# A gated decoder block: w_pool's products among two gates' products, one weight sum per step, first head's blocks issued behind x

## The chip, the cores and the metric

The kernel runs on one core of one Trainium2 chip. The metric is the device time of one launch in microseconds (us), the median of several runs. The engines are named as in the profile: PE (TensorE, matmuls; PEld is its weight load), DVE (VectorE), ACT (ScalarE), POOL (GpSimd) and SP (SyncE, which here only issues transfers).

## The reference

One block of a decoder, sequence 1024, width 1024, all in float32. Cut to what matters:

```python
proj = x @ w_in                                 # 1024 x 7168
q, f_pre, i_val, o_gate, pool_v, gate_a, gate_b = split(proj)
o = hgrn2_chunked(silu(q) * scale, 1 - f, i_val, log(f))      # f from f_pre; 8 heads, chunks of 16
a = (rms_norm(o) * hgrn_norm_g * sigmoid(o_gate)) @ w_a
pooled = causal_multiscale_pool(pool_v)         # trailing means over 2, 4, 8, 16 tokens, minus the token
b = einsum('bsgc,gcd->bsgd', pooled, w_pool) * pool_scale     # 4 groups of 256 columns
merged = sigmoid(gate_a) * a + sigmoid(gate_b) * b
x = LN(alpha * x + merged @ w_out)
x = LN(alpha * x + relu(x @ w_up) ** 2 @ w_down)
```

## The kernel before

**Products.** Every float32 operand is split into a high part, rounded to the fast float32 format of PE (an ACT copy, L125), and a low part, the rest (a DVE subtraction, L126). A product of two such pairs takes three matmuls: L211, L213 and L214 in `prod`, L112, L113 and L114 in `mm3`. Tiles are 128 x 512: sequence halves `u` of 512 tokens, blocks of 128 columns.

**Seven products for eight.** A pair of column blocks of a weight matrix is multiplied with Strassen's scheme in Winograd's form, in `pair`: seven products p1 to p7 instead of eight, of 4 x 3 matmuls each, from sums of weight blocks (b11, b12, b21, b22 and a fifth tile, t) on one side and sums of x on the other. Each step has an operand (t0, b_21, t2, t3, t1, t4, b_22, in that order, which makes the sum and splits it) and a product (p1, p2, p6, p7, p5, p4, p3). Where two pairs run side by side ("twin") the order is another. The sums s1 to s4 of x and their parts (`xp`) stay in SBUF. `takes` say what becomes of the four results.

**Stages.** `head_inputs(h)` makes q and f of a head, `output_gates(h)` the output gates, `pooled(g)` the pooled values of a group (to DRAM, po), `gates(j)` the two gates ga and gb of column block j (to DRAM). They run in the order of the table `ORDER`, one `pair` each. Beside them runs the recurrence of the heads, a generator: `run` calls it once after each product (`next(turning[0])`), and it puts out a piece of a half head. A half head's output is turned (transposes L990, DVE L992 into tile `og`) and written by `put_output`, in part with accumulating stores on POOL's queue (L637).

**The stage in question.** The last in `ORDER` is the sixth gates, `gates(6)`. Behind it stood the four `pool_products(g)` and `gates(7)`. `pool_products(g)` loads w_pool's group and four tiles of pooled values into the ring of six "raw" tiles, which also takes the weight blocks, splits them (group's parts to the rooms q and f, pooled values to the ring "w" of ten), loads gb of the block into one of the rooms v, q, f and og, makes four products of 2 x 3 matmuls, multiplies each with scale and gate (L751) and stores pb. For column block 7, whose gate is not there yet, the scaled product is stored (L749) and `gates(7)` loads it again and multiplies (L722).

**Who sets the order.** The order on PE in this part is the program's own. On the other engines a scheduler of the tile framework sets it, by when operands and tiles are ready in its model and by priorities; every engine then runs its list in order. All loads and most stores are issued by SP, in order: a transfer whose tile is not free yet holds all behind it. A tile of a ring is free when its last reader, a store's landing included, is done.

## Time and profile before

| | us |
|---|---|
| median of three runs | 1473.27 (1473.22 to 1474.59) |
| the profiled execution | 1472.62 |
| its span in the trace | 1470.8 |
| PE busy | 1438.0 |
| DVE busy | 1100.2 |
| ACT busy | 760.8 |

The span is what the trace covers; 1.8 us of the execution's own time lie around it. The sixth gates' first product begins at 600.73 us of the span, w_pool's first at 620.3, the seventh gates' first at 651.43. Views that group or sum the trace name lines of this kernel (L12 is line 12), tiles without their numbers, and count an engine's idle time to what ended it. A matmul is shown with its whole latency of 0.39 us, though the next one may start before it ends.

### The profile page before, as it was taken

Reading aid. Unit: us, or ns where it says so; the run is one execution under the profiler, and the core shown is the slowest. Engines: PE = TensorE matmul, PEld = TensorE weight load, DVE = VectorE, ACT = ScalarE, POOL = GpSimd, SP = SyncE. Lnnn points to the kernel's source line nnn. Section 1 sums busy time; section 2 is a strip of 40 time slices with the busy share of each in tenths; the row PEclk is TensorE's granted clock in tenths of the full one; section 3 lists DMA queues with packets and bytes.
Section 4 is the critical chain, followed back from the end, with each engine's and each line's share of the span. In section 5 each row is a group of like instructions: output and inputs, shape, how many; then the busy total and the mean of one; then the engine's idle time right before and its main releaser. Section 6 shows DMA issues by size and latency. Waiting matters only on the chain.

```text
span 1470.8 us, 20899 instructions
## 1 busy us (share of the span) xinstructions
PE 1438.0 (98%) x7377; PEld 1189.8 (81%) x7377; DVE 1100.2 (75%) x1807; ACT 760.8 (52%) x1383; POOL 107.4 (7%) x288
## 2 busy tenths in 40 slices
PE   8999999999999999979999999999999999999997
PEld 7788888788878888858788878888888888888886
DVE  4967876896897796467985598566666787777977
ACT  5545566665755655545542366555556543333435
POOL 0002111211211210000002100000000100000000
PEclk9999999999999999989999999999999999999999
DMA  7142245345435536797663134444447874435422
GB/s 258 58 136 87 76 127 165 79 137 152 107 93 145 136 87 174 247 337 256 223 230 114 58 100 174 137 154 156 144 151 264 275 263 150 163 131 170 129 72 115
DMA packets 187738, 229.21 MB, mean 156 GB/s; under 512 B 12240, under 2 KB 110576, under 8 KB 187632
## 3 DMA queue, kind: packets, MB, share of 16 engines
q1 hardware_dynamic: 181664, 213.96, 43.9%
q0 software_dynamic: 5184, 11.54, 4.0%
q10 hardware_dynamic: 784, 2.38, 0.5%
q8 instruction: 58, 0.95, 0.3%
q14 instruction: 48, 0.39, 0.1%
HBM read 150.22 MB, written 77.59 MB: 155 GB/s over the span
## 4 chain that ended last, share of the span: by engine, by line
PE 88%; DVE 5%; DMA 4%; issue 1%; ACT 1%; SPq 0%; POOL 0%; DVEq 0%; ACTq 0%
PE ps_pj L211 15%; PE ps_pj L214 15%; PE ps_pj L213 15%; PE ps_pj L1369 4%; PE ps_pj L1367 4%; PE ps_pj L1368 4%; PE ps_pj L112 2%; PE ps_pj L113 2%; PE ps_pj L114 2%; PE ps_tr L1369 1%; PE ps_tr L1367 1%; PE ps_tr L1368 1%; PE ps_sc L211 1%; PE ps_sc L213 1%; PE ps_sc L214 1%
## 5 line engine op out<-in xcount | busy, mean ns | idle before, releaser
L211 PE MATMUL ps_pj<-act,w 128*128 128x512 f32 x1068 | 420.5, 394 | 8.3 <-ACT c L274 2.9
L214 PE MATMUL ps_pj<-act,w 128*128 128x512 f32 x1068 | 416.0, 391 | 2.3 <-DVE w L126 2.3
L213 PE MATMUL ps_pj<-act,w 128*128 128x512 f32 x1068 | 415.3, 390 | 0.0
L125 ACT CAST w<-raw 128x512 fp32r<-128x512 f32 x326 | 202.3, 622 | 289.8 <-PE ps_pj L213 200.9
L126 DVE TENSOR_TENSOR w<-raw,w 128x512 fp32r<-128x512 f32 x326 | 222.8, 686 | 107.2 <-ACT w L125 101.0
L211 PEld LDWEIGHTS ps_pj<-act,w 128*128 128x128 f32 x1068 | 200.9, 188 | 53.6 <-ACT c L274 4.5
L214 PEld LDWEIGHTS ps_pj<-act,w 128*128 128x128 f32 x1068 | 200.8, 188 | 46.4 <-DVE w L126 3.9
L213 PEld LDWEIGHTS ps_pj<-act,w 128*128 128x128 f32 x1068 | 201.0, 188 | 40.5
L1329 ACT CAST act<-act 128x1024 fp32r<-128x1024 f32 x66 | 67.1, 1050 | 109.0 <-issue 35.0
L278 DVE TENSOR_TENSOR c<-c,ps_pj 128x512 f32<-128x512 f32 x95 | 64.7, 682 | 43.5 <-PE ps_pj L214 41.5
L1368 PE MATMUL ps_pj<-act,act 128*128 128x512 f32 x240 | 93.0, 389 | 0.0
L1369 PE MATMUL ps_pj<-act,act 128*128 128x512 f32 x240 | 93.0, 389 | 0.0
L1330 DVE TENSOR_TENSOR act<-act,act 128x1024 fp32r<-128x1024 f32 x66 | 79.4, 1219 | 17.6 <-ACT act L1329 16.5
L1367 PE MATMUL ps_pj<-act,act 128*128 128x512 f32 x240 | 92.5, 389 | 0.0
L274 ACT COPY c<-ps_pj 128x512 f32<-128x512 f32 x96 | 55.9, 582 | 2.5 <-DMA v<-c 1.3
L1368 PEld LDWEIGHTS ps_pj<-act,act 128*128 128x128 f32 x240 | 45.0, 188 | 9.4
L1369 PEld LDWEIGHTS ps_pj<-act,act 128*128 128x128 f32 x240 | 45.0, 188 | 9.4
L1367 PEld LDWEIGHTS ps_pj<-act,act 128*128 128x128 f32 x240 | 45.0, 188 | 9.3
L283 DVE TENSOR_TENSOR raw<-raw,raw 128x512 f32<-128x512 f32 x43 | 29.6, 689 | 28.2 <-DMA raw<-in_w_in_dram 27.1
L1238 ACT ACTIVATE c<-c 128x512 f32<-128x512 f32 x61 | 38.5, 632 | 1.7
L1237 ACT ACTIVATE c<-c 128x512 f32<-128x512 f32 x46 | 29.1, 632 | 16.6 <-DVE c L278 16.4
L1323 DVE TENSOR_TENSOR act<-act,ps_pj 128x512 f32<-128x512 f32 x45 | 30.1, 681 | 6.0 <-PE ps_pj L1369 5.7
(413 smaller groups left out, 2664.2 us busy)
## 6 DMA issues: line engine op xcount, KB each, us to landing
h<-c SPq DMA_DIRECT2D x106, 256.0 KB, 2.7
raw<-in_w_in_dram SPq DMA_DIRECT2D x100, 256.0 KB, 3.2
act<-h SPq DMA_DIRECT2D x78, 256.0 KB, 3.0
draw<-in_w_down_dram SPq DMA_DIRECT2D x16, 1024.0 KB, 7.7
raw<-in_w_up_dram SPq DMA_DIRECT2D x56, 256.0 KB, 2.8
hf<-h SPq DMA_DIRECT2D x34, 256.0 KB, 3.0
s<-og POOLq DMA_DIRECT2D x28, 256.0 KB, 6.1
v<-v SPq DMA_DIRECT2D x16, 256.0 KB, 3.5
```

What stands on the lines that cost most here:

```text
L125: A.copy(hi, src)
L126: V.tensor_sub(lo, src, f(hi))
L211: PE.matmul(ps, wh[:, k], th, start=first and k == 0, stop=False, skip_group_check=True)
L213: PE.matmul(ps, wh[:, k], tl, start=False, stop=False, skip_group_check=True)
L214: PE.matmul(ps, wl[:, k], th, start=False, stop=k == CH - 1, skip_group_check=True)
L274: A.copy(t, ps)
L278: V.tensor_add(t, t, ps)
L1329: A.copy(hi, src)
L1330: V.tensor_sub(lo, src, f(hi))
L1367: PE.matmul(ps, hh[:, w], wh, start=fresh and n == 0, stop=False, skip_group_check=True)
L1368: PE.matmul(ps, hh[:, w], wl, start=False, stop=False, skip_group_check=True)
L1369: PE.matmul(ps, hl[:, w], wh, start=False, stop=n == M - 1, skip_group_check=True)
```

## The change

Three things change.

1. `pool_products` becomes one generator over all groups. While the sixth and seventh gates run, `turning[0]` is `beside(stream, counts)`, which after each of a gate's products steps the remaining recurrence and then as many pool products as `POOL_AFTER` says: 1, 1, 1, 1, 1, 1, 2 in the sixth gates, 2, 2, 2, 2, 0, 0, 0 in the seventh. The tiles come from rooms of the recurrence: w_pool's block to tC, its parts to the ring tD, tE, tF, og, the pooled values to the ring tA, tA, st, st, tH, tH, gb to the four f tiles. The result is in the PSUM tag "tr", two banks. Block 7's scaled products stay in the two v tiles and `gates(7)` multiplies by them there.
2. In `pair`, `make_t2` made two sums in step t2 (L290, L291); now it makes one, and the other is made in step t1, both from other operands than before.
3. The first head's weight blocks are issued behind the last load of x.

```diff
@@ -33,8 +33,9 @@
 ORDER = (
     ("inputs", 1), ("pooled", 0), ("inputs", 2), ("gates", 0), ("output_gates", 2), ("inputs", 3), ("pooled", 1),
     ("inputs", 4), ("output_gates", 4), ("gates", 1), ("inputs", 5), ("pooled", 2), ("inputs", 6), ("output_gates", 6),
-    ("gates", 2), ("inputs", 7), ("pooled", 3), ("gates", 3), ("gates", 4), ("gates", 5), ("gates", 6),
+    ("gates", 2), ("inputs", 7), ("pooled", 3), ("gates", 3), ("gates", 4), ("gates", 5),
 )
+POOL_AFTER = {6: (1, 1, 1, 1, 1, 1, 2), 7: (2, 2, 2, 2, 0, 0, 0)}
 PRIO_WHOLE = 6000
 QUARTER = HALF // 2
 PRIO = 60
@@ -282,14 +283,6 @@
             c["t"] = block_tile() if t is None else t
             V.tensor_sub(c["t"], b22, b12)
 
-        def make_t2():
-            if turned:
-                V.tensor_sub(b12, b11, b12)
-                minus_sum(b11, b22, b12)
-            else:
-                V.tensor_sub(b12, b12, b11)
-                V.tensor_sub(b11, b22, b12)
-
         def t3():
             if twin:
                 make_t3()
@@ -300,6 +293,12 @@
                 make_t3()
                 make_t2()
             return w_part(b11)
+
+        def make_t2():
+            if turned:
+                minus_sum(b11, c["t"], b11)
+            else:
+                V.tensor_add(b11, c["t"], b11)
 
         def t4():
             if twin:
@@ -311,6 +310,10 @@
             return w_part(b21)
 
         def t1():
+            if turned:
+                minus_sum(b12, b22, b11)
+            else:
+                V.tensor_sub(b12, b22, b11)
             return w_part(b12)
 
         def p1(w):
@@ -455,7 +458,7 @@
 
         def load_x(u, w):
             rows_of = x2[u * HALF : (u + 1) * HALF, w].rearrange("(t p) c -> p t c", p=P)
-            nc.sync.dma_start(out=x_rows[u][:, :, w], in_=rows_of)
+            return nc.sync.dma_start(out=x_rows[u][:, :, w], in_=rows_of)
 
         def act_rows():
             return [f(act_tile()) for _ in range(2)]
@@ -486,7 +489,7 @@
         load_x(1, slice(0, HALF))
         load_block(b22, 1, 1)
         load_block(b12, 0, 1)
-        load_x(1, slice(HALF, D))
+        last_x = load_x(1, slice(HALF, D))
         b11, b22, b21, b12 = (rows_of_block(t) for t in blocks)
 
         def parts(rows):
@@ -686,8 +689,10 @@
                     V.scalar_tensor_tensor(t, src, QSCALE, t, ALU.mult, ALU.mult)
                 return take
 
+            with tc.issue_after(last_x.ins) if not h else nullcontext():
+                blocks = loaded_blocks(w_in, h * P, D + h * P)
             run(pair(
-                loaded_blocks(w_in, h * P, D + h * P), (c_soon, c_late, room_f),
+                blocks, (c_soon, c_late, room_f),
                 (take_q(0), take_f(0), take_q(1), take_f(1)),
             ), behind=behind)
 
@@ -710,46 +715,83 @@
             ))
 
         def gates(j):
-            spare = j == KT - 1
-            rooms = [lambda tag=tag: tt(tag) for tag in ("q", "f", "og")] if spare else (c_soon, c_late, c_late)
-
-            def take(dst, src=None, more=None):
+            final = j == KT - 1
+            room = (lambda: tt("q")) if final else c_late
+
+            def take(dst, src=None, u=None):
                 def put(t):
-                    s = (tt("v") if spare else c_late()) if src else t
-                    more_of = loaded(more, lambda: tt("v")) if more is not None else None
+                    s = (tt("og") if final else c_late()) if src else t
                     A.activation(s, t, AF.Sigmoid)
-                    if more_of is not None:
-                        V.tensor_mul(s, s, more_of)
-                    nc.sync.dma_start(out=dst if more is None else more, in_=s)
+                    if final and u is not None:
+                        V.tensor_mul(s, s, held[u])
+                    nc.sync.dma_start(out=pbd[j][u] if final and u is not None else dst, in_=s)
                 return put
 
-            more = pbd[j] if spare else (None, None)
             run(pair(
-                loaded_blocks(w_in, 5 * D + j * P, 6 * D + j * P), rooms,
-                (take(gad[j][0]), take(gbd[j][0], True, more[0]), take(gad[j][1]), take(gbd[j][1], False, more[1])),
+                loaded_blocks(w_in, 5 * D + j * P, 6 * D + j * P), (room if final else c_soon, room, room),
+                (take(gad[j][0]), take(gbd[j][0], True, 0), take(gad[j][1]), take(gbd[j][1], False, 1)),
             ))
 
-        def pool_products(g):
-
-            rooms = iter(("v", "q", "f", "og"))
-            raw = loaded(w_pool[g].rearrange("(k p) c -> p k c", p=P), lambda: block_tile((2, 2 * P)))
-            pods = [[loaded(pod[2 * g + i][u], lambda: block_tile((HALF,))) for i in range(2)] for u in range(2)]
-            parts = iter(("q", "f"))
-            wh, wl = split(raw, lambda: tt(next(parts), F32R).rearrange("p (k c) -> p k c", c=2 * P))
-            for u in range(2):
-                pl = [split(pods[u][i], row_tile) for i in range(2)]
-                for i in range(2):
+        held = [None, None]
+
+        def pool_products():
+
+            def ring(*tags):
+                tags = list(tags)
+                def tile(dtype=F32):
+                    tags.append(tags.pop(0))
+                    return tt(tags[-1], dtype)
+                return tile
+
+            pod_tile, w_tiles = ring("tA", "tA", "st", "st", "tH", "tH"), ring("tD", "tE", "tF", "og")
+
+            def wide(t):
+                return t.rearrange("p (k c) -> p k c", c=2 * P)
+
+            def load(g, u):
+                raw = None
+                if not u:
+                    raw = loaded(w_pool[g].rearrange("(k p) c -> p k c", p=P), lambda: wide(tt("tC")))
+                return raw, [loaded(pod[2 * g + i][u], pod_tile) for i in range(2)]
+
+            def parts(g, u, raw, pods):
+                if raw is not None:
+                    w_parts[g] = split(raw, lambda: wide(w_tiles(F32R)))
+                return [split(t, row_tile) for t in pods]
+
+            w_parts = {}
+            todo = [(g, u) for g in range(CH) for u in range(2)]
+            soon = [load(*todo[0]), load(*todo[1])]
+            pl = parts(*todo[0], *soon.pop(0))
+            yield
+            for n, (g, u) in enumerate(todo):
+                if n + 2 < len(todo):
+                    soon.append(load(*todo[n + 2]))
+                wh, wl = w_parts[g]
+                for i in (0, 1) if g < CH - 1 else (1, 0):
                     w = slice(i * P, (i + 1) * P)
                     j = 2 * g + i
-                    tag = next(rooms)
-                    t = tt(tag) if j == KT - 1 else loaded(gbd[j][u], lambda: tt(tag))
-                    ps = ps_tile()
+                    final = j == KT - 1
+                    t = tt("v") if final else loaded(gbd[j][u], lambda: tt("f"))
+                    ps = ps_tile("tr", 2)
                     mm3(ps, [(wh[:, c, w], wl[:, c, w], *pl[c]) for c in range(2)])
-                    if j == KT - 1:
+                    if final:
+                        held[u] = t
                         A.activation(t, ps, AF.Copy, scale=pscale[:, j : j + 1])
                     else:
                         V.scalar_tensor_tensor(t, ps, pscale[:, j : j + 1], t, ALU.mult, ALU.mult)
-                    nc.sync.dma_start(out=pbd[j][u], in_=t)
+                        nc.sync.dma_start(out=pbd[j][u], in_=t)
+                    if i == (1 if g < CH - 1 else 0) and soon:
+                        pl = parts(*todo[n + 1], *soon.pop(0))
+                    yield
+
+        def beside(stream, counts):
+
+            for n in counts:
+                next(turns, None)
+                for _ in range(n):
+                    next(stream, None)
+                yield
 
         def pooled(g):
 
@@ -1040,12 +1082,14 @@
                     head_inputs(j)
                 else:
                     dict(gates=gates, pooled=pooled, output_gates=output_gates)[what](j)
+            stream = pool_products()
+            next(stream)
+            for j, counts in POOL_AFTER.items():
+                turning[0] = beside(stream, counts)
+                gates(j)
             for _ in turns:
                 pass
-            for what, j in (
-                ("pool_products", 0), ("pool_products", 1), ("pool_products", 2), ("pool_products", 3), ("gates", 7),
-            ):
-                dict(gates=gates, pool_products=pool_products)[what](j)
+            turning[0] = iter(())
 
 
         hg_scope.close()
```

What it moves, at three places. On PE, where the sixth gates' first product (ps_pj_1214 before, ps_pj_1225 now) ends and the second begins; `ps_tr` is a pool product, `tD` and `tE` are w_pool's high and low part, `w` the parts of weights or pooled values. Before:

```order
L211 MATMUL ps_pj_1214_6505<-act_22_216,w_1212_6501 128x512
L213 MATMUL ps_pj_1214_6505<-act_22_216,w_1212_6501 128x512
L214 MATMUL ps_pj_1214_6505<-act_22_216,w_1213_6502 128x512
L211 MATMUL ps_pj_1219_6525<-act_32_241,w_1216_6520 128x512
L213 MATMUL ps_pj_1219_6525<-act_32_241,w_1216_6520 128x512
```

and now:

```order
L215 MATMUL ps_pj_1225_6527<-act_22_216,w_1224_6524 128x512
L113 MATMUL ps_tr_1231_6550<-w_1214_6506,tD_1212_6502 128x512
L114 MATMUL ps_tr_1231_6550<-w_1215_6507,tD_1212_6502 128x512
L115 MATMUL ps_tr_1231_6550<-w_1214_6506,tE_1213_6503 128x512
L113 MATMUL ps_tr_1231_6550<-w_1216_6510,tD_1212_6502 128x512
L114 MATMUL ps_tr_1231_6550<-w_1217_6511,tD_1212_6502 128x512
L115 MATMUL ps_tr_1231_6550<-w_1216_6510,tE_1213_6503 128x512
L212 MATMUL ps_pj_1235_6564<-act_32_241,w_1232_6559 128x512
```

The six matmuls of a pool product, which stood behind all of the sixth gates, stand between two of their products.

On DVE now, in the middle of the sixth gates: L127 makes low parts (of w_pool where it reads tC, of pooled values where tA, of gates' weights where raw), L782 multiplies a pool product by scale and gate, L279 and L284 are sums of `pair`:

```order
L127 TENSOR_TENSOR w_1262_6687<-raw_1221_6519,w_1261_6686 128x512
L127 TENSOR_TENSOR og_1256_6674<-tC_1227_6542,tF_1255_6673 128x512
L782 TENSOR_SCALAR f_1253_6662<-ps_tr_1254_6664,prm_120,f_1253_6662 128x512
L127 TENSOR_TENSOR w_1269_6724<-raw_1219_6516,w_1268_6723 128x512
L127 TENSOR_TENSOR w_1273_6754<-tA_1246_6626,w_1272_6753 128x512
L279 TENSOR_TENSOR c_1252_6660<-c_1252_6660,ps_pj_1225_6527 128x512
L127 TENSOR_TENSOR w_1275_6758<-tA_1247_6628,w_1274_6757 128x512
L284 TENSOR_TENSOR raw_1293_6822<-raw_1295_6825,raw_1294_6823 128x512
L782 TENSOR_SCALAR f_1266_6711<-ps_tr_1267_6713,prm_120,f_1266_6711 128x512
L127 TENSOR_TENSOR tE_1286_6807<-tC_1263_6705,tD_1285_6806 128x512
L279 TENSOR_TENSOR c_1245_6624<-c_1245_6624,ps_pj_1234_6563 128x512
L127 TENSOR_TENSOR w_1277_6762<-raw_1222_6521,w_1276_6761 128x512
```

The second row, w_pool's second low part, goes into the room `og`, which the last half head's output held; behind it stand the gates' low part of p4 (w_1269) and, behind w_pool's third low part (tE_1286), that of p3 (w_1277). None of the pool's rows stood among the sixth gates' before.

On SP now, from the same part of the program (f<-gb loads a gate, pb<-f stores a product, tC<-in_w_pool_dram loads w_pool's third and fourth block, tA<-po pooled values, raw<-in_w_in_dram a weight block of the seventh gates, gb6 a finished gate):

```order
L783 DMA pb0_1_984<-f_1248_6630 128x512
L223 DMA raw_1295_6825<-in_w_in_dram 128x4x128
L618 DMA tC_1263_6705<-in_w_pool_dram 128x2x256
L783 DMA pb1_1_986<-f_1253_6662 128x512
L618 DMA tA_1301_6848<-po6_0_979 128x512
L618 DMA f_1281_6784<-gb2_1_956 128x512
L618 DMA tA_1302_6850<-po7_0_981 128x512
L727 DMA gb6_1_964<-c_1252_6660 128x512
L618 DMA f_1283_6795<-gb3_1_958 128x512
L783 DMA pb2_0_987<-f_1266_6711 128x512
L618 DMA tC_1300_6846<-in_w_pool_dram 128x2x256
```

Loads that need a product's store to have landed first (f_1281 takes the tile of f_1248) now stand ahead of w_pool's and other blocks on the queue, where before the pool's transfers stood behind the sixth gates' blocks and ahead of the seventh's.

## The prediction

> **What bounds the kernel now.** First the page: TensorE (PE) is busy for all but 33 us of the span, and the chain that ended last runs over it.
>
> ```profile
> span 1470.8 us, 20899 instructions
> PE 1438.0 (98%) x7377; PEld 1189.8 (81%) x7377; DVE 1100.2 (75%) x1807; ACT 760.8 (52%) x1383; POOL 107.4 (7%) x288
> PE 88%; DVE 5%; DMA 4%; issue 1%; ACT 1%; SPq 0%; POOL 0%; DVEq 0%; ACTq 0%
> ```
>
> So an edit gains only what it takes from PE's idle or slow time. The table of stretches (span, then busy time and count for each engine, granted clock, DMA share, GB/s) tells where that lies:
>
> ```profile
> core 0: us, PE busy (x) PEld busy (x) DVE busy (x) ACT busy (x) POOL busy (x), PEclk, DMA share, GB/s
> 600.00:620.00 20.00, 20.00 (x91) 16.55 (x91) 8.77 (x13) 10.54 (x18) 2.63 (x3) 1.00 0.85 240
> 620.00:640.00 20.00, 17.76 (x70) 13.64 (x70) 12.34 (x18) 7.30 (x12) 0.00 (x0) 0.91 1.06 401
> 640.00:660.00 20.00, 15.04 (x56) 10.88 (x54) 14.37 (x23) 9.81 (x18) 0.00 (x0) 0.91 0.87 305
> 660.00:680.00 20.00, 19.67 (x80) 16.11 (x81) 14.92 (x24) 10.95 (x21) 0.00 (x0) 0.91 0.58 185
> ```
>
> The sixth gates' products end by 620.4 without a loss. Then come w_pool's products and the seventh gates, where PE is idle for 2.24 + 4.96 + 0.33 = 7.5 us and its clock is down. In steps of 5 us:
>
> ```profile
> 630.00:635.00 5.00, 2.76 (x10) 1.68 (x9) 3.52 (x6) 2.08 (x4) 0.00 (x0) 0.89 1.06 402
> 635.00:640.00 5.00, 5.00 (x18) 3.70 (x17) 1.96 (x3) 1.21 (x2) 0.00 (x0) 0.77 1.06 406
> 640.00:645.00 5.00, 3.05 (x12) 2.19 (x11) 3.97 (x7) 2.51 (x5) 0.00 (x0) 0.91 1.07 394
> 645.00:650.00 5.00, 4.22 (x13) 2.94 (x13) 2.61 (x4) 1.19 (x2) 0.00 (x0) 0.75 1.10 368
> 660.00:665.00 5.00, 4.67 (x13) 3.70 (x14) 5.00 (x9) 3.27 (x7) 0.00 (x0) 0.66 0.82 245
> ```
>
> Lost clock is (0.11 + 0.23) x 5 = 1.7 us, (0.09 + 0.25) x 5 = 1.7 and 0.34 x 5 = 1.7: three dips of 1.7 us each, one after each of the larger stops. Their releasers, by the waits of PE from 600 to 720:
>
> ```profile
> PE ps_pj L112 <- ACT q L125: 2.2, 1, 2.2
> PE ps_pj L112 <- DVE q L751: 2.0, 1, 2.0
> PE ps_pj L211 <- ACT w L125: 1.5, 1, 1.5
> PE ps_pj L214 <- DVE w L126: 1.0, 1, 1.0
> ```
>
> And the chain through them, which shows what stands behind the two engines named (start, duration, what):
>
> ```profile
> 626.63 4.84 DMA raw<-po
> 636.77 5.21 DMA f<-gb
> 642.33 0.76 DVE q L751
> ```
>
> The pool products wait for operands that come from DRAM too late: pooled values into six "raw" tiles, gates into whichever result tile is free. Transfers run at 406 GB/s and a share above 1 at the same time.
>
> **What the stage loses.** Matmul starts stand 0.227 us apart (2.50 us over 11 steps of the sixth gates' first product), and these are the rows for the counts:
>
> ```profile
> 600.73 0.39 PE L211 MATMUL ps_pj<-act,w 128*128 128x512 f32 x1
> 603.23 0.39 PE L214 MATMUL ps_pj<-act,w 128*128 128x512 f32 x1
> 606.18 0.60 PE L990 MATMUL ps_tr<-ident,tH 128*128 128x128 f32 x4
> L112 PE MATMUL ps_pj<-w,q x32: 389/389/628, 620.3 to 650.8; 128*128 128x512 f32 x32
> 651.43 0.39 PE L211 MATMUL ps_pj<-act,w 128*128 128x512 f32 x1
> ```
>
> w_pool's products are 3 x 32 = 96 matmuls, so 21.8 us; they took 651.4 - 620.3 = 31.1, a loss of 9.3. The seventh gates lose the waits of 1.5 and 1.0, 0.16 more at each (a matmul counts as busy 0.39, but the next could start after 0.227), and one dip: 4.5. Together **13.8 us**. Nothing is computed more or less afterwards, so this is the most that this part can bring.
>
> **Part one: the products among the gates.** Both gates are 7 x 12 = 84 matmuls each; with the 96 and four transposes (0.4) the stage is 264 x 0.227 + 0.4 = 60.3 us of pure work, from 600.7 to 661.0. I laid this schedule out product by product: one of w_pool's (6 matmuls, 1.36 us) after each of the sixth gates' (2.72 us), two after each of the first four of the seventh. Operands now have 4.1 us a product, not 1.36, and go to rooms that the recurrence has left; the first can be loaded before 620, where the DMA share is 0.85 and not 1.06. For pb7 two stores and two loads of 256 KB fall away: 1.05 MB, 2.6 us of transfers at 400 GB/s. That takes away the cause of the four waits. The counts of splits, drains and sums do not change. What is late next:
>
> *The room og.* w_pool's second low part is written into og, which holds the last half of the recurrence's output until its accumulating stores have landed.
>
> ```profile
> L637 POOL DMA_DIRECT2D s<-og x3: 859/1206/1548, 608.1 to 609.2; - x3
> DMA to landing us min/median/max: 7.8/9.2/10.6
> ```
>
> In the profile the last lands at about 609.2 + 10.6 = 619.8. Now a product stands ahead of the transposes (1.36 later): 621.1. VectorE (DVE) then needs 0.69 for the part: 621.8. The schedule wants it for the fifth product's third matmul at 620.65. Stall **1.1**. Bounds: 0, if they land as early as the min of 7.8, and about 3, if transfers crowd them. All that follows on DVE's queue waits too, among it the fourth product's drain and the low part of gates' p4, which come in at 623.2, just when PE, late itself, asks for them.
>
> *w_pool's third block.* Its load reuses the room that this same part reads, so it is issued only at 621.8. Landings (w_in's over the whole run, w_pool's from 620 to 650, the slowest gate's from 600 to 630) and the two halves of a split:
>
> ```profile
> raw<-in_w_in_dram SPq DMA_DIRECT2D x100, 256.0 KB, 3.2
> raw<-in_w_pool_dram SPq DMA_DIRECT2D x1, 256.0 KB, 5.2
> f<-gb SPq DMA_DIRECT2D x1, 256.0 KB, 7.5
> L126 DVE TENSOR_TENSOR w<-raw,w 128x512 fp32r<-128x512 f32 x32 | 21.7, 689 | 17.2 <-ACT w L125 16.7 <-PE ps_pj L113 0.4
> L125 ACT CAST w<-raw 128x512 fp32r<-128x512 f32 x33 | 20.2, 619 | 28.2 <-DMA raw<-po 10.5 <-PE ps_pj L213 10.5 <-PE ps_pj L113 2.2
> ```
>
> It lands at 627.0; ScalarE (ACT) splits it to 627.6, and only then makes the high part of gates' p3 (628.2), since that stands behind it in ACT's order. On DVE the low part of w_pool (628.3), a sum (0.69) and p3's low part follow (629.7). PE reaches p3 at 626.8, with the first stall: it waits 1.4 for the first matmul and 1.0 for the third. Stall **2.4**; bounds 0.5 (it lands after 3.2, as w_in's blocks do) and 5 (after 7.5).
>
> *The clock.* 2.4 us in two pieces is what the pair 1.5 + 1.0 was before, and that pair was followed by a dip. I count one dip, **1.7**; bounds 0 and two dips. The Trainium skill ("TensorE: Matmul & The Clock Gate", Part 1, and its section on HAM oscillation) has the clock halve only after an idle window of about 3.4 us and gives the rule that gaps over that length are to be avoided; by it these stalls would cost no clock and the sum would be 1.7 us lower. No idle stretch in the rows above is longer than 2.2 us, and yet there are three dips, so I go by the rows.
>
> *The rest.* DVE is the engine with least room here (14.9 of 20 us in the busiest stretch); single low parts come up to some tenths late: **0.5**, bounds 0 and 2.
>
> So 13.8 - 1.1 - 2.4 - 1.7 - 0.5 = **8.1 us** gained.
>
> **Part two: weight sums one per step.** As many sums as before, but one of two leaves the place ahead of t2's split and stands ahead of t1's. It only matters where DVE's order holds PE:
>
> ```profile
> PE ps_pj L211 <- ACT c L274: 2.9, 2, 1.5
> PE ps_pj L214 <- DVE w L126: 2.3, 3, 1.0
> 260.00:265.00 5.00, 3.86 (x18) 2.85 (x16) 4.78 (x11) 4.94 (x11) 0.27 (x3) 1.00 0.02 7
> 285.00:290.00 5.00, 4.29 (x19) 3.19 (x17) 5.00 (x13) 4.25 (x10) 3.54 (x10) 1.00 0.18 52
> 256.70 0.58 DVE raw L290
> ```
>
> The two waits for L274 lie in these two stretches (and left the clock whole); the chain into the first runs over the sum at L290 (0.58), which goes. 2 x 0.6 = **1.2 us**. Elsewhere on the recurrence's DVE runs the sum that moves to t1 can cost the same once or twice: bounds +1.2 lost and 3 gained (if the waits for low parts outside of the stage, 2.3 - 1.0 = 1.3, go too). Everywhere else PE has no idle time, and an earlier part gains nothing.
>
> **Part three: the first head's blocks behind x.** The first 40 transfers on SP's queue stand in the same order with and without it: 0.
>
> **Sum.** 8.1 + 1.2 = 9.3 off the profiled execution's 1472.6: 1463.3. That execution is 0.65 below the median of the runs, so **1463.9** is the forecast.
>
> **Rivals.** *Clean* (chance 0.22): accumulating stores and w_pool's block arrive in time, no dip. For it: the transfers are spread out and 1.05 MB fewer. Gain 13.8 - 0.5 + 1.2 = 14.5, so 1458; with 3 us at the sums, 1456.
>
> *Transfers stay the bound* (0.15).
>
> ```profile
> DMA packets 8456, 11.83 MB, mean 394 GB/s; under 512 B 707, under 2 KB 3654, under 8 KB 8455
> ```
>
> That is 620 to 650. From 600 to 675 the stretches add up to 240 x 20 + 401 x 20 + 305 x 20 + 185 x 15 = 21.7 MB; without 1.05 it is 20.6, at 394 GB/s 52 us of the 60.3. That fits with little to spare, and a queue in order loses some: a second stall pair and dip (2.5 + 1.7) leave 1468. The Trainium skill ("DMA: Bandwidth & Descriptors", "Where 436 GB/s comes from") has transfers between HBM and SBUF bound by about 358 GB/s: 58 us for the same bytes, which would make this rival likelier. The 394 GB/s held over 30 us disagree with that.
>
> *Slower* (0.13): the ring of gate tiles. Four "f" tiles carry all products: load of a gate, product, DVE (0.75), store, and only then the next load, which SP issues in order ahead of w_in's, w_a's and w_pool's blocks.
>
> ```profile
> pb<-f SPq DMA_DIRECT2D x3, 256.0 KB, 5.2
> f<-gb SPq DMA_DIRECT2D x2, 256.0 KB, 5.6
> ```
>
> A round is 0.75 + 5.2 + 5.6 = 11.6 us. Four products take 16.4 in the sixth gates, but 2 x 2.72 + 4 x 1.36 = 10.9 in the seventh: 0.7 short a round, which two PSUM banks partly cover. If landings are 8 us, the round is 16.75 and loses 2 x 5.9 + 2 x 0.4 = 12.5, with two dips 15.9; with the 3.5 of the stalls above that is 4.4 more than the 13.8 + 1.2 removed: 1477.6. It decides from about 7.3 us a landing. For it: the gate's 7.5 and the accumulating stores' 9.2. Against it: those are of the fullest stretch, and the loads of the first four come long ahead.
>
> *No change* (0.07): stalls and dips add up to within 3 us of what they were, 1472. That the change does not do what it says is excluded: in its order the products stand where it says.
>
> **Numbers.** 0.2% of the time, 2.9 us, is what a measurement of this kernel tells from none. Forecast 0.43 (its own range 1460 to 1467), clean 0.22, transfers 0.15, none 0.07, slower 0.13. Faster: 0.43 + 0.22 + 0.15 = 0.80. The range from 1456 (clean, with the sums' best) to 1472 leaves out the slower case and a few of none.
>
> **What would show it.** In the changed profile PE should be at full rate from 600 to about 620; a wait of about 1 us near 621 for DVE's og, and a wait of 1 to 2.5 near 627 at p3 for ACT and DVE, with the clock down in one stretch behind it; none of 2 us between 630 and 660; the seventh gates' end near 667. Without the waits at og and w_pool's third block, clean is right; waits behind gate loads or stores in the seventh gates speak for the slower rival. The two waits for L274 should shrink to about 0.9 each. The forecast is wrong if the recurrence's last rooms come free later than 600, or if the next stage, whose operands now are needed some 8 us earlier, stalls for what is gained.

## The result, and the profile after

| | before | changed |
|---|---|---|
| median (6 runs each, in turn) | 1473.42 | 1465.88 |
| lowest to highest | 1472.57 to 1475.53 | 1462.77 to 1468.74 |
| profiled execution | 1472.62 | 1466.59 |
| its span | 1470.8 | 1464.9 |

The ratio is 0.9947, with a 95% interval of 0.9933 to 0.9960: 7.5 us less by the medians, 5.9 to 9.9 by the interval. The forecast was 1463.9, 9.4 below the median it started from.

The page of the changed kernel. The chain that ended last still runs over PE, and 29.4 us of the span lie outside of PE's busy time where it was 32.8:

```profile
span 1464.9 us, 20840 instructions
PE 1435.5 (98%) x7377; PEld 1188.4 (81%) x7377; DVE 1100.1 (75%) x1807; ACT 759.0 (52%) x1383; POOL 107.6 (7%) x288
PE 87%; DVE 6%; DMA 4%; issue 1%; ACT 1%; SPq 0%; DVEq 0%; POOL 0%; ACTq 0%
```

The stretches of the stage (columns as in the prediction). Lines in this part of the changed kernel have numbers one higher than before: splits are L126 and L127, products L212, L214 and L215, drains L275 and L279.

```profile
600.00:620.00 20.00, 19.84 (x89) 16.00 (x88) 9.38 (x14) 9.84 (x17) 2.62 (x3) 1.00 0.75 208
620.00:640.00 20.00, 17.17 (x67) 13.28 (x66) 13.90 (x22) 7.02 (x13) 0.00 (x0) 0.91 0.99 340
640.00:660.00 20.00, 19.52 (x84) 15.54 (x84) 16.29 (x26) 13.78 (x25) 0.00 (x0) 1.00 0.80 270
660.00:680.00 20.00, 20.00 (x90) 16.56 (x89) 16.87 (x27) 10.31 (x19) 0.00 (x0) 1.00 0.85 274
680.00:700.00 20.00, 16.74 (x70) 12.59 (x69) 13.10 (x22) 10.50 (x19) 0.00 (x0) 1.00 0.92 313
630.00:635.00 5.00, 4.70 (x14) 3.71 (x15) 2.40 (x5) 1.76 (x4) 0.00 (x0) 0.66 1.03 347
```

From 640 to 680, where PE had been idle for 5.3 us and slowed twice, it is now idle for 0.5 and at full clock. One hole is left at 620 to 640, with one dip of the clock, (1 - 0.66) x 5 = 1.7 us; and a hole of 3.3 us has opened at 680 to 700, in the next stage (the products with w_a), which begins at 668.1 behind the seventh gates. The waits of PE from 595 to 720 (total, times, longest) name both:

```profile
PE ps_pj L212 <- ACT w L126: 2.2, 1, 2.2
PE ps_hg L212 <- ACT act L131: 2.1, 1, 2.1
PE ps_pj L215 <- DVE w L127: 1.3, 3, 0.7
```

The first and one of the third are p3 of the sixth gates, at 626.5 to 630.3. The second is an operand of the next stage, at 686.7.

**Lost time.** To compare profiles I use one sum: from the start of each matmul to the start of the next, what exceeds the pitch (0.227 us for 512 columns, less for narrow ones). It holds stops, dips of the clock (stretches at a lower granted clock) and small delays alike. Where many narrow matmuls run, outside of the stage, its level depends on the pitch taken for them, so there only the differences between kernels are read.

| us lost in the profile | 100-180 | 260-300 | 600-680 | 680-720 | 850-885 | all |
|---|---|---|---|---|---|---|
| before | 1.9 | 5.3 | 14.3 | 1.6 | 5.5 | 66.2 |
| changed | 1.0 | 5.0 | 7.1 | 5.0 | 3.4 | 60.5 |

The stage gained 7.2 and the next one gave back 3.3. The difference of the two sums, 5.7, is that of the spans, 5.9.

**The stop at p3.** The chain of waits through it (start, duration, what), and the issues of SP at that place (start, duration of the issue, line, what):

```profile
612.66 8.25 DMA pb<-f
620.98 0.32 SPq L618
621.35 3.59 DMA pb<-f
```

```profile
618.93 0.47 SPq L618 DMA_DIRECT2D tH<-po  x1
620.98 0.32 SPq L618 DMA_DIRECT2D f<-gb  x1
621.35 0.42 SPq L783 DMA_DIRECT2D pb<-f  x1
621.86 0.38 SPq L223 DMA_DIRECT2D raw<-in_w_in_dram  x1
622.30 0.67 SPq L618 DMA_DIRECT2D tC<-in_w_pool_dram  x1
```

A product's store needed 8.25 us to land. The gate load f<-gb that takes its tile waited for it at the head of SP's queue from 619.4 to 620.98, and w_pool's third block (tC), three places behind, went out at 622.30. On ACT (start, duration, line, what, and in brackets the idle time before it):

```profile
627.71 0.62 ACT L126 CAST tD<-tC 128x512 fp32r<-128x512 f32 x1 [3.37 <-DMA tC<-in_w_pool_dram]
628.23 0.61 ACT L126 CAST w<-raw 128x512 fp32r<-128x512 f32 x1
```

ACT was idle for 3.37 us in front of that block, with the high part of p3 (w<-raw, whose operand was there) behind it. That is the order in its list, not a lack of ACT.

**The stop at 686.7.** SP's issues there:

```profile
676.42 0.32 SPq L727 DMA_DIRECT2D pb<-og  x1
677.39 5.89 SPq L618 DMA_DIRECT2D ga<-ga  x4
683.69 0.32 SPq L618 DMA_DIRECT2D c<-o  x1
```

The seventh gates' last result stands in `og` and is stored at 676.42. The next stage's tile `ga` lies over that room, so its load waits until the store has landed, at 682.0, and holds SP's queue (5.89 us for a row that otherwise takes some 0.4 a transfer). Behind it stands c<-o, the operand that PE asks for at 686.7; it goes out at 683.69. The view blames ACT, which splits this operand, but the cause is a store and a queue in order.

### The profile page after: what moved, and what is told of

Its sections match the earlier page's. It is cut to its first block, busy times and chain, and to the rows that moved or that the text cites. A ratio compares the mean times of both kernels' runs of the same rounds, so it can differ in the third digit from the quotient of the medians.

```text
span 1464.9 us, 20840 instructions
## 1 busy us (share of the span) xinstructions
PE 1435.5 (98%) x7377; PEld 1188.4 (81%) x7377; DVE 1100.1 (75%) x1807; ACT 759.0 (52%) x1383; POOL 107.6 (7%) x288
## 4 chain that ended last, share of the span: by engine, by line
PE 87%; DVE 6%; DMA 4%; issue 1%; ACT 1%; SPq 0%; DVEq 0%; POOL 0%; ACTq 0%
PE ps_pj L212 15%; PE ps_pj L215 14%; PE ps_pj L214 14%; PE ps_pj L1412 4%; PE ps_pj L1413 4%; PE ps_pj L1411 4%; PE ps_pj L114 2%; PE ps_pj L113 2%; PE ps_pj L115 2%; PE ps_tr L1412 1%; PE ps_tr L1413 1%; PE ps_tr L1411 1%; PE ps_sc L215 1%; DVE w L127 1%; PE ps_hg L215 1%
## 5 line engine op out<-in xcount | busy, mean ns | idle before, releaser
L212 PE MATMUL ps_pj<-act,w 128*128 128x512 f32 x1068 | 420.2, 395 | 10.8 <-ACT c L275 3.3
L215 PE MATMUL ps_pj<-act,w 128*128 128x512 f32 x1068 | 415.7, 391 | 1.3 <-DVE w L127 1.3
L214 PE MATMUL ps_pj<-act,w 128*128 128x512 f32 x1068 | 415.0, 390 | 0.0
L126 ACT CAST w<-raw 128x512 fp32r<-128x512 f32 x310 | 192.5, 622 | 278.1 <-PE ps_pj L214 201.7
L127 DVE TENSOR_TENSOR w<-raw,w 128x512 fp32r<-128x512 f32 x310 | 212.1, 686 | 92.8 <-ACT w L126 87.6
L212 PEld LDWEIGHTS ps_pj<-act,w 128*128 128x128 f32 x1068 | 200.7, 188 | 56.9 <-ACT c L275 4.6
L215 PEld LDWEIGHTS ps_pj<-act,w 128*128 128x128 f32 x1068 | 200.8, 188 | 45.2 <-DVE w L127 2.6
L214 PEld LDWEIGHTS ps_pj<-act,w 128*128 128x128 f32 x1068 | 200.8, 188 | 40.8 <-DVE act L132 0.2
L279 DVE TENSOR_TENSOR c<-c,ps_pj 128x512 f32<-128x512 f32 x95 | 64.8, 682 | 39.1 <-PE ps_pj L215 35.6
L275 ACT COPY c<-ps_pj 128x512 f32<-128x512 f32 x96 | 55.8, 581 | 3.1 <-issue 1.8
L284 DVE TENSOR_TENSOR raw<-raw,raw 128x512 f32<-128x512 f32 x43 | 29.6, 690 | 33.2 <-DMA raw<-in_w_in_dram 28.8
```

The source lines that it names most:

```text
L126: A.copy(hi, src)
L127: V.tensor_sub(lo, src, f(hi))
L212: PE.matmul(ps, wh[:, k], th, start=first and k == 0, stop=False, skip_group_check=True)
L214: PE.matmul(ps, wh[:, k], tl, start=False, stop=False, skip_group_check=True)
L215: PE.matmul(ps, wl[:, k], th, start=False, stop=k == CH - 1, skip_group_check=True)
L275: A.copy(t, ps)
```

## The experiments

All are edits of the changed kernel except e8, which is one of the kernel before. Each chip ran the kernel before beside them. The ratio can lie up to 0.001 off the quotient of the two medians; gains are told by the ratio unless medians are named. Losses in a stretch are those of one profiled execution of each kernel. Three of these lie well off their median: e1 (1471.02) and e11 (1468.27) above it, e7 (1462.40) below.

| | median | before, beside it | ratio (95%) |
|---|---|---|---|
| e1_v_part | 1466.80 | 1476.22 | 0.9946 (0.9927 to 0.9964) |
| e2_gate_queue | 1466.00 | 1476.22 | 0.9935 (0.9920 to 0.9950) |
| e3_v_and_queue | 1465.14 | 1476.22 | 0.9927 (0.9911 to 0.9944) |
| e4_f_room | 1465.56 | 1476.22 | 0.9937 (0.9921 to 0.9953) |
| e5_p3_first | 1466.37 | 1475.46 | 0.9944 (0.9925 to 0.9963) |
| e6_p3_first_f_room | 1464.83 | 1475.46 | 0.9934 (0.9917 to 0.9952) |
| e7_plain_stores | 1464.18 | 1475.46 | 0.9931 (0.9911 to 0.9952) |
| e8_sums_only | 1470.19 | 1475.46 | 0.9971 (0.9956 to 0.9985) |
| e9_after_again | 1467.43 | 1475.63 | 0.9948 (0.9933 to 0.9963) |
| e10_no_sums | 1472.04 | 1475.63 | 0.9976 (0.9962 to 0.9991) |
| e11_both_blocks_early | 1464.82 | 1475.63 | 0.9930 (0.9917 to 0.9942) |
| e12_next_stage_behind | 1465.28 | 1473.87 | 0.9946 (0.9930 to 0.9961) |

### e1: w_pool's second low part to a free room

```diff
-ring("tD", "tE", "tF", "og")
+ring("tD", "tE", "tF", "v", "tD", "tE", "tF", "og")
```

> The changed kernel, with one edit: w_pool's second low part goes to a v tile instead of og, so it no longer waits for the accumulating stores. The changed profile has a stop of PE at 626.3 ahead of the sixth gates' p3 (2.3 us, released by ACT), 0.8 more at p3's third matmul (released by DVE), and a dip of 1.7: 4.9 us together. Theory 'room og': the late landing in og held w_pool's third block, and all of it followed; now the block loads from about 618, the stop goes and so does the dip: about 1461. Rival 'queue': SP was held until 621.0 by the load of a gate into an f tile whose store (pb1, issued 612.7) had not landed, and behind it stood the weight block raw_1295 (issued 621.9, landed 627.0) that a sum on DVE waits for, ahead of p3's low part. Then the stop only changes its releaser: ACT's part is early, DVE's low part of p3 still comes at about 629.4, a wait of some 2 us at p3's third matmul, with or without a dip: 1464 to 1466.

The stop at p3 went; a larger one came at 618.7, worth 4.3 us, with a dip behind it, and the stage lost some 9 us. PE's wait, and ACT behind it:

```profile
PE ps_pj L212 <- ACT w L126: 4.1, 1, 4.1
```

```profile
621.60 0.62 ACT L126 CAST w<-tH 128x512 fp32r<-128x512 f32 x1 [10.18 <-DMA tH<-po]
```

The pooled values in tH were issued at 612.5 and landed at 621.5, 9 us later; ACT stood idle for 10.2 us in front of them, and p5's part behind. The median is that of the changed kernel. So the room og was one of several things due at about 621, not the one that holds PE.

### e2: the gate loads on another queue

```diff
-loaded(gbd[j][u], lambda: tt("f"))
+loaded(gbd[j][u], lambda: tt("f"), nc.gpsimd)
```

> The changed kernel, with one edit: the pool products' gates (f tiles) are loaded on POOL's queue instead of SP's, so that no wait for a store's landing holds SP. w_pool's second low part stays in og. Theory 'room og': w_pool's third block can still be loaded only from 621.2 on (its room is read until then), lands at about 626.5, ACT's p3 part is ready at 627.7 and DVE's at about 629: PE stops about 1.1 and 0.5 to 1 us at p3, perhaps with a dip: 1463 to 1465. Rival 'queue': the stop goes, about 1461. A third way: loads on POOL's queue land later (accumulating stores there took 7.7 to 10.6 us), the gate tiles come late and the seventh gates stall: 1468 and more.

SP was no longer held and w_pool's block came in time. Now the room og was last, as the prediction had it, only larger:

```profile
PE ps_tr L115 <- DVE og L127: 2.1, 1, 2.1
```

The stage lost 6.6 (7.1 in the changed kernel), a dip of the clock included.

### e3: both

The edits of e1 and e2 together:

```diff
-ring("tD", "tE", "tF", "og")
+ring("tD", "tE", "tF", "v", "tD", "tE", "tF", "og")
...
-loaded(gbd[j][u], lambda: tt("f"))
+loaded(gbd[j][u], lambda: tt("f"), nc.gpsimd)
```

> Both edits of the two runs before in one kernel. If the stop at p3 has these two causes and no third, it is gone whichever theory holds, with its dip: PE loses under 1 us between 620 and 640 and the time is about 1461. If each edit alone already gives 1461, the causes were not independent; if the stop stays with both, DVE's own backlog makes it.

No dip in the stage, but 6.3 us lost: 2.3 at 628.6 where p3's low part stood on DVE behind a weight sum whose block, raw, took 8.4 us to land (issued 620.1, there at 628.5), and 1.0 twice from 642 to 650. With both suspects away, a third late landing took the place.

### e4: the seventh gates' result not under the next stage's tile

```diff
-s = (tt("og") if final else c_late()) if src else t
+s = (tt("f") if final else c_late()) if src else t
```

> The changed kernel, with one edit: the seventh gates' last result (gate b of the first half) stands in an f tile and not in og. In the changed profile PE stops 2.3 us at 686.7, in the stage behind, for ACT's part of the operand act<-c; SP stood from 677.8 to 682.0 ahead of a load into a tile ga that lies over og, whose store (pb7, issued 676.4) landed then, and the operand's load stood behind it. Theory 'tile over og': without it the operand's load goes out 4 us earlier and the stop is gone: 2.3 us less, about 1463.6. Rival 'transfers': the stretch from 690 to 705 runs at a DMA share of 1.03 to 1.10, so what is gained at 686.7 comes back at the stop at 698.3 (1.15 us, the profile before had 1.5 there): no more than 1 us less, about 1465.

The stretch behind the seventh gates in this run, against 16.74 busy in the changed kernel:

```profile
680.00:700.00 20.00, 18.93 (x82) 15.01 (x81) 15.78 (x26) 12.75 (x23) 0.00 (x0) 1.00 1.06 374
```

The stop at 686.7 is gone; 680 to 720 lost 2.2 instead of 5.0. That shows its cause. How much it costs grows, roughly, with the time that the store needs to land: in the versions that keep `og`, SP was held for it by 4.1 us (e9), 3.7 (e1), 2.9 (e3 and e5) and 2.4 (e2), and PE stopped behind it for 1.6, 1.4, 0.4 and 0.9, and 0.3. In the medians the 2.8 us are not seen clearly: the ratio is 0.001 (1.5 us) below that of the changed kernel, inside the intervals.

### e5: p3's parts ahead of w_pool's third block

On ACT and DVE the split of w_pool's third block and the seventh gates' first sum were put behind p3's parts.

```diff
-w_parts[g] = split(raw, lambda: wide(w_tiles(F32R)))
+with behind_parts("p3") if g == 2 else nullcontext():
+    w_parts[g] = split(raw, lambda: wide(w_tiles(F32R)))
...
-make_t3()
-make_t2()
+with tc.issue_after(made_last["p3"]) if sums_late[0] else nullcontext():
+    make_t3()
+    make_t2()
```

> The changed kernel, with one edit of the order: the split of w_pool's third block (ACT's high part, DVE's low part) and the seventh gates' first weight sum on DVE are issued behind the parts of the sixth gates' p3; all transfers and rooms stay. The two runs with another room and another queue moved the stop but did not end it: landings from 612 to 621 take 7 to 9 us, so whatever stands in order behind one of them is late. Theory 'order of the parts': p3's own operand has been in SBUF since before 610, and it only waits because late blocks stand ahead of it on ACT and DVE. With it ahead, the 2.3 + 0.8 at p3 and the dip of 1.7 go, 4.9 less than the changed kernel. Rival 'only moved': the blocks that land at 627 and 628 now hold the seventh gates' p1 and the pool products behind it, and 2 us or more come back between 630 and 640.

No stop at p3. Instead:

```profile
PE ps_pj L212 <- ACT w L126: 2.9, 1, 2.9
```

This one is at 637.2, in the seventh gates' p2. On ACT:

```profile
636.71 0.62 ACT L126 CAST tF<-tC 128x512 fp32r<-128x512 f32 x1 [4.95 <-PE ps_tr L114]
639.25 0.62 ACT L131 CAST act<-c 128x512 fp32r<-128x512 f32 x1 [1.40 <-DMA c<-o]
639.78 0.61 ACT L126 CAST w<-raw 128x512 fp32r<-128x512 f32 x1
```

The part of p2 (w<-raw) stood behind two late operands: w_pool's fourth block (tC), issued at 632.1 and landed at 636.7, and then c<-o, an operand of the next stage, for which ACT stood idle for another 1.40 us. The second is the one that ended the stop. With 1.7 more at 646.7 the stage lost 7.0. The stop had only moved to the next late operands on ACT's list.

### e6: e4 and e5 together

e5's lines, and

```diff
-s = (tt("og") if final else c_late()) if src else t
+s = (tt("f") if final else c_late()) if src else t
```

> The order of the run before together with the f tile for the seventh gates' last result (which ended the 2.3 us at 686.7). If both act on different waits they add: 4.9 + 2.3 to 2.8 less than the changed kernel, a ratio of about 0.990 to the kernel before. If the next stage is bound by its transfers, being 5 us earlier there brings a new stop of 1 to 3 us between 670 and 700, and the sum is not reached.

The next stage lost 1.7, the stage 7.5: the stop was 3.3 at 638.8, again at p2 and again ended by c<-o (landed at 641.1), and two dips followed. The time is e4's and e5's within their intervals.

### e7: plain stores instead of accumulating ones

The last half head's three stores on POOL's queue, issued from 610 to 611, write and do not add. What this kernel leaves out is the earlier terms of the sums s1, s2 and s4 in that block, so it does not compute the block's result; it is run for its times alone:

```diff
-nc.gpsimd.dma_start(out=osd[name][kp], in_=t, accum_op=ALU.add)
+nc.gpsimd.dma_start(out=osd[name][kp], in_=t)
```

> The changed kernel, but the last half head's three stores on POOL's queue write and do not add (so the sums of head outputs s1, s2 and s4 lack all earlier terms in the last block; the bytes written are the same, the reading that adding needs falls away). Theory 'accumulating stores hold the DMA engines': at 615 to 620 the DMA share is 1.10 at only 276 GB/s, where 626 to 640 of the kernel before had 1.06 at 406. With plain stores pb1's landing falls from 8.3 to about 5 us, og is free by 617, SP goes on 2 to 3 us earlier and the stop at p3 falls from 3.2 to under 1.5 us. Rival 'burst of loads': eight loads and stores in a row from 610 to 618 fill the engines anyway; landings stay at 7 us or more and the stop stays above 2.

Landings of these stores, by the table of transfers issued from 600 to 630 (count, KB, median us to landing), in the changed kernel and here:

```profile
s<-og POOLq DMA_DIRECT2D x3, 256.0 KB, 7.7
```

```profile
s<-og POOLq DMA_DIRECT2D x3, 256.0 KB, 5.2
```

And the stretch in which they run, in the changed kernel and here, then the one after it here:

```profile
615.00:620.00 5.00, 5.00 (x24) 4.10 (x23) 2.05 (x3) 2.82 (x6) 0.00 (x0) 1.00 1.10 276
```

```profile
615.00:620.00 5.00, 5.00 (x24) 4.10 (x23) 3.46 (x7) 2.23 (x5) 0.00 (x0) 1.00 1.05 363
620.00:640.00 20.00, 19.33 (x84) 15.35 (x83) 15.01 (x25) 9.83 (x18) 0.00 (x0) 1.00 1.01 347
```

With the DMA engines as full as before, 363 GB/s go through instead of 276. The store that had held SP landed in 5.55 us instead of 8.25, the stop at p3 shrank from 3.2 to 0.8, no dip came, and the stage lost 3.6. This is the one edit that shortened the late landings themselves, and the only single edit after which no stop over 1.2 us was left in the stage. The next stage still lost 4.3, and in the medians the gain over the changed kernel stays inside the intervals.

### e8: the weight sums alone

The kernel before with part two and nothing else:

```diff
 def make_t2():
     if turned:
-        V.tensor_sub(b12, b11, b12)
-        minus_sum(b11, b22, b12)
+        minus_sum(b11, c["t"], b11)
     else:
-        V.tensor_sub(b12, b12, b11)
-        V.tensor_sub(b11, b22, b12)
+        V.tensor_add(b11, c["t"], b11)
...
 def t1():
+    if turned:
+        minus_sum(b12, b22, b11)
+    else:
+        V.tensor_sub(b12, b22, b11)
     return w_part(b12)
```

> The kernel before with part two alone: one weight sum in t2, the other in t1. My step of the prediction: 1.2 us less, from the two stops at 263 and 289, each 0.6 shorter. Rival, from the changed profile: there the stop at 263 is 0.44 shorter, that at 289 0.1 longer, those at 432 and 436 together 0.4 longer and those between 864 and 877 1.9 shorter, so about 2 us less and nearly all of it at 864 to 877. A third way: all of these are shifts from run to run, and the time is the same within 1 us. Nothing changes from 600 to 680, where 13 to 14 us stay lost.

4.3 us faster (2.2 to 6.5) where the prediction had 1.2 for this part. Of the two waits on which I had placed it, the one at 263 shrank as forecast (1.48 lost before, 0.96 here), the one at 289 grew (1.70 and 2.31); together they did not move. Its profile shows less loss at 850 to 885 (5.5 to 3.9), where three of the waits for low parts are gone: before,

```profile
PE ps_pj L214 <- DVE w L126: 1.3, 2, 1.0
PE ps_hg L211 <- ACT w L125: 0.8, 1, 0.8
PE ps_hg L214 <- DVE w L126: 0.7, 1, 0.7
```

and with the sums moved,

```profile
PE ps_pj L211 <- ACT c L274: 0.8, 1, 0.8
PE ps_pj L211 <- ACT w L125: 0.5, 1, 0.5
```

This run shows one thing more. Its products stand as they did before the change, yet the stretches 600 to 680 and 680 to 720 differ; before, and here:

```profile
600.00:680.00 80.00, 72.47 (x294) 57.18 (x294) 50.40 (x77) 38.61 (x67) 2.63 (x3) 0.94 0.84 283
680.00:720.00 40.00, 38.65 (x171) 31.56 (x170) 35.85 (x60) 21.76 (x39) 0.00 (x0) 1.00 0.79 264
```

```profile
600.00:680.00 80.00, 73.41 (x315) 57.84 (x314) 53.27 (x84) 39.30 (x69) 2.62 (x3) 1.00 0.87 293
680.00:720.00 40.00, 36.87 (x153) 29.46 (x152) 33.52 (x56) 20.26 (x37) 0.00 (x0) 0.96 0.75 256
```

Here the old order of products ran without any of the three dips (0.06 x 80 = 4.8 us); and the next stage, reached sooner, lost 5.6 us instead of 1.6, a dip among it: PE stopped at 685.9 for a weight's part that stood on ACT behind the split of an operand c<-o, issued at 681.73 and 5.23 us under way. So dips are not a fixed property of an order, and in this profile what the stage gained the next one gave back, with none of the changed rooms. The 3.0 us by which its span is shorter than that of before are mostly not the sums' either: its clock stayed whole in the first 20 us (0.91 before), and the hundredth matmul starts 2.2 us sooner.

### e9: the changed kernel once more

No edit; it stands beside e10 and e11 on their chip.

> The changed kernel once more, on the chip of the two runs beside it, so that they are compared with it and not with another chip's runs. The first measurement gave 0.9947 of the kernel before (0.9933 to 0.9960), 7.5 us less; the same is expected within its interval. In the profile: a stop of about 3 us at the sixth gates' p3, one of about 2 us at 687 and between none and three dips of the clock, since the runs of one kernel so far differ by whole dips of 1.7 us.

0.9948, as the first time (0.9947). Lost: 6.8 in the stage, 4.7 in the next. The picture of the first profile holds.

### e10: the products alone

The changed kernel with the sums of part two as they were:

```diff
-        minus_sum(b11, c["t"], b11)
+        V.tensor_sub(b12, b11, b12)
+        minus_sum(b11, b22, b12)
     else:
-        V.tensor_add(b11, c["t"], b11)
+        V.tensor_sub(b12, b12, b11)
+        V.tensor_sub(b11, b22, b12)
...
 def t1():
-    if turned:
-        minus_sum(b12, b22, b11)
-    else:
-        V.tensor_sub(b12, b22, b11)
     return w_part(b12)
```

> The changed kernel with part two undone: both weight sums in t2 again. The run of the sums alone took 0.9971 of the kernel before, 4.3 us less (2.2 to 6.5), where my prediction had 1.2. If the sums are worth that much, this kernel is 3 to 5 us slower than the changed one beside it. If they are worth the 1.2 of the prediction, or the 2 us that the stretches of the changed profile show, it is 1 to 2 us slower, and the 4.3 was in part the luck of fewer dips. The other part alone is then worth about 6 of the 7.5 us, against 3 in the first case.

3.6 us faster than before (1.3 to 5.6), and by the medians 4.6 slower than e9 on the same chip. So of the 8.2 us there, the products brought 3.6 and the sums 4.6, and e8 agrees with the second. The loss at 100 to 180 (2.1) is that of before. At 850 to 885 the size is that of before (5.7), but not what it is made of. Of the four waits two are back,

```profile
PE ps_hg L212 <- ACT w L126: 0.8, 1, 0.8
PE ps_hg L215 <- DVE w L127: 0.7, 1, 0.7
```

and behind them, at 870, stands a dip of 1.7 us that the profile of before did not have there. Another follows the wait at 263, which is back with 1.99 lost. So the old place of the sums brings back the wait at 263 and one of the three for low parts; the other two are not shown to be the sums' doing.

### e11: w_pool's late blocks loaded early

e4 and e5's sum, and the third and fourth block into rooms free long before:

```diff
-lambda: wide(tt("tC"))
+lambda: wide(tt("tC" if g < 2 else "v"))
```

> The changed kernel with three edits: w_pool's third and fourth block are loaded into the two v tiles (free from about 595) instead of tC, which is free only when the second block's low part is made, the seventh gates' first sum on DVE is issued behind p3's parts, and the seventh gates' last result stands in an f tile. With p3's parts put first in the earlier run, the stop came back at 637 as 3.1 us, where ACT's part of w_pool's fourth block (load issued at 632.1) stood ahead of the seventh gates' p2. Theory 'one room for w_pool's blocks': the late loads are what stands in order ahead of others; with both blocks in SBUF before 612 the stops at p3 and at 637 go, and with the f tile that at 687: PE loses under 4 us from 600 to 720 (12.1 in the changed kernel), so 6 to 8 us less than it. Rival 'stores and queue': the gate loads behind unfinished stores still hold SP from 619 to 621, late weight blocks of the seventh gates make the same stops at other places, and no more than 3 us are gained.

Nothing worth a microsecond stopped PE up to 638; then

```profile
PE ps_pj L212 <- ACT w L126: 5.6, 1, 5.6
```

at 638.8: the seventh gates' p2 part stood on ACT behind the split of the next stage's operand, issued at 637.4 and landed at 642.4. That is again an operand c<-o, as in e5. Two dips followed, and the stage lost nearly 9 us in this profile. The median is 2.6 us below e9's, the intervals overlap.

### e12: the next stage's operands behind the seventh gates'

e11, and on ACT and DVE the first two operands of the next stage behind p5's parts:

```diff
-split_into(xp[name][kp], loaded(src, c_tile))
+t = loaded(src, c_tile)
+with behind_parts("p5") if name in ("a11", "a12") else nullcontext():
+    split_into(xp[name][kp], t)
```

> The kernel of the run before (both w_pool blocks early, first sum behind p3, f tile), with one edit more: the parts of the next stage's first two operands (a11 and a12, eight splits each on ACT and DVE together) are issued behind the part of the seventh gates' p5. In the run before, PE lost about 1 us from 600 to 638 and then 5.8 us at 638.8, where ACT's part of the seventh gates' p2 stood behind the split of an operand that the next stage needs 25 us later and whose load (issued 637.4) landed at 642.4. Theory 'order behind a late landing': this stop goes as well, no dip follows, and PE loses under 5 us from 600 to 720: 4 to 6 us less than the run before, a ratio of about 0.989 to 0.990. Rival 'DVE is full': from 640 to 665 it is busy 85% and more, the moved splits now hold p4's part or the next stage, and the stop appears at 655 or at 664 with 2 us or more.

```profile
600.00:620.00 20.00, 20.00 (x91) 16.28 (x90) 10.50 (x16) 10.05 (x17) 2.63 (x3) 1.00 0.81 230
620.00:640.00 20.00, 20.00 (x89) 16.30 (x88) 15.47 (x25) 9.12 (x16) 0.00 (x0) 1.00 0.93 319
640.00:660.00 20.00, 18.70 (x82) 14.98 (x81) 14.38 (x23) 11.14 (x21) 0.00 (x0) 1.00 0.88 291
680.00:700.00 20.00, 16.65 (x61) 11.92 (x60) 13.88 (x23) 12.99 (x24) 0.00 (x0) 0.91 1.04 357
```

From 600 to 640 PE has no idle time; the stage loses 4.1 of the 14.3 it lost before. The next one now loses 6.5, a dip among it, and the time is the changed kernel's. Its products begin at 663.3, 4.8 us sooner than in the changed kernel, but the operands c<-o are issued from 675.8 to 677.9 and need a median of 6.0 us to land; PE stops at 681.0 for the split of one of them. The loss was pushed out of the stage and did not leave the kernel.

No version was faster than the changed kernel by more than the intervals tell.

## Why the prediction held, and where it did not

**The total** was right within 2 us, and inside the range of the likeliest case alone. Its terms were not: part one brought 3.6 (e10; 1.3 to 5.6) and not 8.1, part two 4.3 (e8; 2.2 to 6.5) and not 1.2. Two errors cancelled, and that the total fits is luck. (The rival clean was summed from the profiled execution and not from the median, so its 1458 and 1456 stand 0.65 low.)

**Part one, in its own stage.** The prediction took 8.1 from 13.8; the profile shows 7.2 from 14.3. Term by term:

- *The room og*, 1.1 predicted: 0. The accumulating stores landed by 620.4 and DVE's part started at 620.52, where 621.1 was predicted; PE asked for it at 621.5. The mechanism was there: with SP freed (e2) it cost 2.1 us.
- *w_pool's third block at p3*, 2.4 predicted: 2.33 at the first matmul and 0.84 at the third, 3.2. Place, order on ACT and the two pieces were as predicted. What released the load was not: it could have gone at 621.2 by its room, and went at 622.30 because SP was held by a gate load behind a store of 8.25 us. That hold is worth at most 1.1 of the 3.2 us; the room, late itself, would have held the load until 621.2 in any case. This is the mechanism of the rival that I called slower, the ring of gate tiles, for one round; the stores issued from 600 to 630 took 4.6 us in the median, under the 7.3 from which I had let it decide.
- *The clock*, one dip of 1.7: one dip of 1.7 in this profile and in e9's; e4, with the same two stops, has none, and e10 two.
- *The rest*, 0.5: about 2, with 0.6 at 648.4, 0.3 at 609.8, and the rest spread thin.
- PE's full rate from 600 to 620, no stop of 2 us from 630 to 660 and the seventh gates' end (668.1 for 667) came as said.

**The step that failed** is the one that stood in the prediction only as a condition: that the next stage would take the stage's 8 us as they came. It gave 3.3 back in the profile, and the products alone brought 3.6 us (e10) where the sum had 8.1. The direct cause of the new stop is shown (e4): a result in `og` under the tile `ga`, and SP in order behind it. But behind that seems to lie something wider. e8 gave back 4 of 4.8 us in the old layout, and e12, which nearly emptied the stage of stops, paid in the next. From 600 to 700 the transfers take 0.75 to 0.99 of the DMA engines in every stretch of 20 us of the changed kernel. PE's work there was brought forward, and the bytes were not: 281 GB/s over these 100 us, 28.1 MB, where the kernel before moved 292, 29.2 MB, of which the change drops 1.05. That the transfers are the bound of the next stage is argued from this and not shown. Against it stands e4: without the held queue 374 GB/s went through from 680 to 700 instead of 313, and 680 to 720 lost 2.2. The rival that called transfers the bound may have had the cause in part, though it placed the loss in the stage and put the whole at 1468.

**Part two**, 1.2 predicted: 4.3 alone, 4.6 undone. The mechanism (one sum less ahead of a split on DVE) is borne out at one place: the wait at 263 lost 1.48 and 1.99 with the sums in the old place (before, e10), and 1.04, 0.96 and 1.07 with them moved (changed, e8, e9). That at 289 did not shrink (1.70 and 1.84; 1.78, 2.31 and 1.67). The size was too small: I gave nothing to "the waits for low parts outside of the stage" except in a bound, and nothing to the clock. In the profiles with the sums moved, 850 to 885 lost 3.4 to 3.9 instead of 5.5 to 5.7, though 1.7 of the latter is e10's dip. At 100 to 180 the changed kernel lost 1.0 and e8 1.6, instead of 1.9 to 2.1. Against that, 300 to 340 lost 1.0 to 1.4 us more. That is a net of 0.5 us in e8 and 2 in the changed kernel. The granted clock of the runs gives about 1.3 more: (1 - mean clock) x 1470 is 8.2 us in e8 and 9.5 in the runs of before beside it. The other 1 to 2.5 us of the 4.3 I cannot place; the interval goes down to 2.2.

**Part three**, 0: the first 40 transfers on SP's queue stand in the same order in both profiles, so nothing is seen that it could move. It was not run by itself, so that it is worth nothing is not shown.

**Late landings** are the root of what is left in the stage. Shown: with plain stores (e7) the landings grew shorter and the stop at p3 shrank to 0.8 us. That no dip came there shows nothing, since e4 had the whole stop without one. Shown as well: taking away what waits for a late landing, one or two at a time (e1, e2, e3, e5, e11), put the stop at the next one, since SP, ACT and DVE run their lists in order and each had another late operand a few places on.

**The clock was priced by luck as much as by rows.** The runs of one kernel differ by whole dips: the 17 runs of before beside e5 to e8 went from 1469.66 at a mean clock of 0.997 to 1478.82 at 0.990, so 1.3 us for each 0.001. The same two stops at p3, 2.3 to 2.5 and 0.8 to 1.2 us, stand in four profiles; one dip followed in the changed kernel and in e9, none in e4, two in e10. Elsewhere a stop of 2.3 us was followed by one dip (e2), one of 3.3 by two (e6), 3.1 and 1.7 by none (e5), and the 2.3 at 686.7 in the changed kernel by none. The Trainium skill ("TensorE: Matmul & The Clock Gate", on HAM oscillation) gives gaps over some 3.4 us as those to avoid; here dips came behind shorter ones, so its bound did not hold for this kernel, and no other length parts the cases either. By the granted clock, dips cost the kernel before 8.7 to 10.4 us a run on the chips used, the changed kernel 5.6 and 7.1; on the chip of e9, where both stand side by side, 10.3 and 7.1. Not all of that is the stage's: in the profile before, three dips of 1.7 lie in the stage, and the rest in the first 20 us (mean clock 0.91) and the last 21 (0.90), where the changed kernel has it too. The difference says that some 3 us of the gain go with dips that no longer come.

## What to carry to other kernels

When a stage is made shorter, price the next one as if its operands came no sooner than now: which loads feed it, what its tiles lie over, and what stands ahead of them on a queue in order. Where several landings are late at once, moving one waiter only shows the next; look for what makes them late (here three accumulating stores). And measure the parts of a change alone: a total that fits can hide two terms that are both wrong.
